# Three pad tiles between SBUF pools, and a state space recursion by pairs and fours, in a two-block network kernel

## The chip, the cores and the metric

The kernel runs on one core of a Trainium2 chip. One launch computes everything. The metric is the device time of one execution in microseconds (us); 1,995.99 us is the median of three runs before the change (1,995.98 to 1,996.63).

## The reference

The input is a sequence of 256 tokens with 1,024 features, in float32. A first block has a state space mixer with a gated projection, a squared-ReLU MLP and a gated additive projection. A second block of two layers has four mixers side by side (Fourier, convolution, grouped attention, differential attention) over the sequence and a context of 256 tokens, each followed by a SwiGLU MLP. Cut to what the change touches:

```python
def s5_mixer(u, ...):                      # u: (1, 256, 1024), 64 groups of 16 features, 64 complex states each
    ab = exp(lam * dt)                     # complex, per group and state
    bu = einsum('blgh,gph->blgp', ug, bb)  # input to each state
    xs = scan over l:  xs[l] = ab * xs[l-1] + bu[l]
    y  = real(einsum('blgp,ghp->blgh', xs, c)) + d_skip * u
    a, g = split(gelu(y) @ w_glu)
    return a * sigmoid(g)

def sqrelu_mlp(h, w1, w2):  a = relu(h @ w1); return (a * a) @ w2
def swiglu(h, w1, w3, w2):  return (silu(h @ w1) * (h @ w3)) @ w2
```

## The kernel before

**The projections.** Activations are kept with the features on the 128 partitions and the tokens along the row. Each float32 operand is split into a high part (rounded to the type that TensorE multiplies in one pass, `fp32r`) and a low part. A product takes three matmuls for each 128 features: high weights by high activations (L363), high by low (L364), low by high (L365), all in `mm3`; `mm3x` (L372 to L374) does the same for two units in turn. The weights come by DMA into `ws` tiles, are split by ScalarE (L331) and VectorE (L332) into `wh` and `wl` of pool `wr`, and are the stationary operand; 256 or 512 tokens move. In the token projections (`tok_wide`, L1029 to L1031) it is the other way round: activations are stationary and 512 weight columns move.

**Where tiles lie.** `run` opens the pools one after another, and each lies behind the one before in every partition: `c`, `sm`, `p1` (tiles `k1`, 1,024 bytes), `p2` (`k2`, 2,048 bytes), `p4` (`k4`, 4,096 bytes). Then the pools of the state space stage are opened and closed, and in their place come `ws` (3 tiles of 4,096 bytes), `wr` (4 each of `wh` and `wl`, 4,096 bytes), `up` (one tile of 4 x 286 floats), `ph` (`h4`, six of 4,096 bytes) and `late`. `Act` is the class of activations with a high and a low part; it takes its tiles from `k4` unless told otherwise. From `k4` come `y`, `h` and `g` of the first block, all `m`, and the mixers' results `zg`, `z`, `zd`, `zc`. From `ph` come `hc` of the first layer and `hx` of both; the `h` of the two SwiGLUs has its high parts in `ph` and its low parts in `k4`.

**The state space stage.** The 256 tokens are 32 chunks of 8. Within a chunk a Toeplitz matrix (`kt`, spread by 32 transfers into `mt`) gives the output (L739); across chunks the state at each chunk's start is needed. `s5_params` computes the powers of `ab`. `b_outer` builds the products that turn a chunk of inputs into its state contribution, PE applies them (L660) and ScalarE copies the contributions into `zb` (L670). A loop of 30 steps then runs the recursion across chunks on VectorE, four instructions a step on 2 x 32 columns (L677 to L680), with copies that swap the real and imaginary halves of `zb` after steps 23 and 30 (L686 to L688). `c_outer` builds the tap products `ca` on VectorE (L780, L782) and GpSimd (L781, L782); PE makes `kt` from them (L708, L714), ScalarE copies it (L716), SP and GpSimd issue the `mt` transfers (L720). Last, `zb` times `ca` is added to the output (L751).

**Order.** The program is written in the order of the functions; the framework's scheduler places each engine's instructions by program order and by when it takes their inputs to be ready, so `c_outer` and the recursion are interleaved on VectorE. L739 is held before L751 with `issue_after`, and the first loads behind the stage (`ple_proj`) are issued after the last `mt` transfer on SP.

Of the kernel before, what the change touches and what calls it, by code (L numbers as in the profile page):

```python
# [9 lines left out]
F32 = mybir.dt.float32  # L10
# [3 lines left out]
ALU = mybir.AluOpType  # L14
# [3 lines left out]
P = 128  # L18
# [260 lines left out]
class Net:  # L279
# [216 lines left out]
    def s5_params(self):  # L496
# [80 lines left out]
                f, g = slice(64 * half, 64 * half + 64), slice(32 * half, 32 * half + 32)  # L577
                self.S.copy(self.bb3[r, g, 0::2], bb[f, ri].unsqueeze(2).to_broadcast([64, 32, 2, 16]))

        arr, aii = (self.q6.tile([P, 2, 32], F32, name=s) for s in ("arr", "aii"))  # L580
        for r in range(2):
            V.tensor_copy(arr[:, r, :], pr[:, :, 0])
        V.tensor_scalar(aii[:, 0, :], pi[:, :, 0], -1.0, None, op0=ALU.mult)
        V.tensor_copy(aii[:, 1, :], pi[:, :, 0])
        self.arr, self.aii = arr, aii

    def b_outer(self, dst, g0, xr, xi):

# [15 lines left out]
    def s5(self):  # L604
# [13 lines left out]
        sh = [P, 32, 32]  # L618
# [20 lines left out]
        for h in range(2):  # L639
            G.memset(mt[h], 0.0)  # L640
        zb = self.q6.tile([P, 2, 32, 32], F32, name="zb")
        V.memset(zb[:, :, :, 0:1], 0.0)
        bre, bim = self.bb[:, 0], self.bb[:, 1]
        for jp in range(4):
            ss_sb = self.k4([P, 2, 2, 2, 64], F32, "ss")
            for jj in range(2):
                pt = self.q4.tile([P, 4, 2, 8, 16], F32, tag="pt", name=self.nm("pt"))
                self.b_outer(pt, (jp * 2 + jj) * 4, bre, bim)
                self.ada_next(2)
                pmt = self.k4([P, 4, 2, P], F32, "pmt")  # L650
                for g2 in range(2):
                    ps = self.pm([P, 4, P])
                    for i in range(4):
                        g4, ri = g2 * 2 + i // 2, i % 2
                        T.transpose(ps[:, i, :], pt[:, g4, ri].rearrange("p s h -> p (s h)"), self.ident)
                    S.copy(pmt[:, g2 * 2 : g2 * 2 + 2].rearrange("p a b c -> p (a b) c"), ps)
                ps = self.px([P, 2, 2, 64])
                for half in range(2):
                    for g4 in range(4):
                        T.matmul(ps[32 * g4 : 32 * g4 + 32, half], u2[half][:, g4 * 8 + jp * 2 + jj, :],  # L660
                                 pmt[:, g4, :, half * 64 : half * 64 + 64], start=True, stop=True)
                S.copy(ss_sb[:, jj], ps.rearrange("p a b c -> p b a c"))
            ps = self.px([P, 2, 2, 4, 32])
            for jj in range(2):
                for ri in range(2):
                    T.transpose(ps[:, jj, ri].rearrange("p a b -> p (a b)"),
                                ss_sb[:, jj, ri].rearrange("p a b -> p (a b)"), self.ident)
            for jj in range(2):
                g0 = (jp * 2 + jj) * 4
                S.copy(zb[:, :, g0 : g0 + 4, 1:32], ps[:, jj, :, :, 0:31])  # L670


        for s in range(1, 31):
            prev, nxt = zb[:, :, :, s], zb[:, :, :, s + 1]
            t1 = self.sm([P, 2, 32])
            t2 = self.sm([P, 2, 32])
            V.tensor_tensor(t1, prev, self.arr, op=ALU.mult)  # L677
            V.tensor_tensor(t2, zb[:, ::-1, :, s], self.aii, op=ALU.mult)
            V.tensor_tensor(t1, t1, nxt, op=ALU.add)
            V.tensor_tensor(nxt, t1, t2, op=ALU.add)  # L680
            if s in (23, 30):

                c = slice(0, 24) if s == 23 else slice(24, 32)
                t = self.bb.rearrange("p a (b e) c -> p (a b) (e c)", e=2)
                cp = V.tensor_copy if s == 23 else S.copy
                cp(t[64:128, :, c], zb[0:64, 1, :, c])  # L686
                V.tensor_copy(zb[0:64, 1, :, c], zb[64:128, 0, :, c])
                cp(zb[64:128, 0, :, c], t[64:128, :, c])  # L688


        ca = {}
# [1 line left out]
        for j in range(8):  # L693
            c = self.k4([P, 8, 8, 16], F32, "ca")
            for g0 in (0, 4):
                self.c_outer(c[:, g0 : g0 + 4], j * 8 + g0, c1, c2)
            self.ada_next()
            ca[j] = c


        for half in range(2):
# [40 lines left out]
        for half in range(2):  # L742
            y = ysb[half] = self.k4([P, 8, 8, 16], F32, "ysb")
            for jq in range(2):
                ps = pss[half, jq]
                with self.tc.issue_after(last.ins):
                    for j4 in range(4):
                        j = jq * 4 + j4
                        for g4 in range(4):
                            g = j * 4 + g4  # L750
                            T.matmul(ps[32 * g4 : 32 * g4 + 32, j4].rearrange("p s h -> p (s h)"), zb[:, half, g, :],  # L751
                                     ca[half * 4 + g // 8][:, g % 8].rearrange("p s h -> p (s h)"), start=False, stop=j4 == 3)
                (V.tensor_copy if jq else S.copy)(y[:, :, jq * 4 : jq * 4 + 4].rearrange("p s j h -> p j s h"), ps)
        S.copy(self.x[:, 0, 0:1], ysb[0][:, 0, 0, 0:1])
# [845 lines left out]
    def run(self):  # L1600
        tc, nc = self.tc, self.nc
        V, S, G = self.V, self.S, self.G
        with ExitStack() as st:
# [4 lines left out]
            self.ps_ = pool("sm")  # L1608
            self.p1 = pool("p1")
            self.p2 = pool("p2")  # L1610
            self.p4 = pool("p4")
            self.psm = pool("psm", 3, space=PSUM)
            self.psx = pool("psx", space=PSUM)
# [32 lines left out]
                nc.scalar.dma_start(self.rope.rearrange("p a b c -> p (a b c)"), self.a["rope"])  # L1646
            self.stage, self.ada_off = self.k4, 0
            self.ws = pool("ws", 3)
            self.wr = pool("wr", 4)
            self.up = pool("up", 1)  # L1650
            self.ph = pool("ph", NH)
            pl = pool("late")
            self.late = {"k4a": pl, "k1c": pl, "k1g": pl}
# [115 lines left out]
```

## Time and profile before

| | |
|---|---|
| median of three runs | 1,995.99 us |
| profiled execution | 1,997.63 us |
| its span, first to last instruction | 1,995.9 us |
| PE busy | 96% |
| DVE busy | 78% |
| ACT busy | 46% |
| POOL busy | 7% |
| mean granted TensorE clock | 0.985 of full speed |
| DMA | 162 GB/s on average |

PE is TensorE, DVE VectorE, ACT ScalarE, POOL GpSimd, SP the engine that issues most transfers. A matmul's duration runs from its issue to its modelled end, and the next one starts before it ends; so the distance between two starts is the time that one takes in the stream, and the duration is not. Where a line of the timeline ends in brackets, they hold the idle time ahead of it and what ended it.

### The profile page before, as it was taken

What the parts mean: (1) busy time and instruction counts of PE and PEld (TensorE: products, weight loads), DVE (VectorE), ACT (ScalarE), POOL (GpSimd) and SP (SyncE); (2) the same over time, 40 slices, a digit from 0 to 9 for tenths busy, and PEclk for the clock granted to TensorE, in tenths of its full rate; (3) what the DMA queues carried; (4) which work ended last, traced back from release to release, by engine and by line L of the source; (5) the groups of instructions that cost most, each with busy time, mean ns of one, the idle gap of its engine ahead of it and who ended that gap; (6) DMA issues with size and microseconds to landing.
All of it is one profiled execution on the core that took longest, in us unless ns stands there. A gap on an engine that the chain in (4) does not pass through costs nothing.

```text
span 1995.9 us, 35545 instructions
## 1 busy us (share of the span) xinstructions
PE 1906.2 (96%) x13842; PEld 1692.7 (85%) x13842; DVE 1548.6 (78%) x3133; ACT 927.4 (46%) x1583; POOL 130.9 (7%) x138
## 2 busy tenths in 40 slices
PE   3869999999999999999999999999999999999998
PEld 1457899998789998789998777787998789999997
DVE  9974577699987789998778576675689997776665
ACT  2443445455654555664553212212555664544443
POOL 6720000000000011000000000000100000010000
PEclk8989999999999999999999999999999999999998
DMA  5657665554345564236555455454455235555663
GB/s 176 187 187 244 224 199 183 180 183 156 106 125 169 182 191 156 88 106 189 181 187 157 126 163 164 152 165 124 141 178 157 74 108 170 180 180 169 183 187 107
DMA packets 103192, 323.45 MB, mean 162 GB/s; under 512 B 16416, under 2 KB 18608, under 8 KB 102640
## 3 DMA queue, kind: packets, MB, share of 16 engines
q1 hardware_dynamic: 102256, 319.53, 51.3%
q8 instruction: 109, 1.79, 0.4%
q0 software_dynamic: 336, 1.44, 0.2%
q14 instruction: 59, 0.48, 0.1%
q10 hardware_dynamic: 432, 0.21, 0.0%
HBM read 317.47 MB, written 1.05 MB: 160 GB/s over the span
## 4 chain that ended last, share of the span: by engine, by line
PE 84%; DVE 11%; issue 2%; DMA 2%; ACT 1%; SPq 0%; DVEq 0%; ACTq 0%
PE pm L363 21%; PE pm L364 21%; PE pm L365 21%; PE pm L1029 2%; PE pm L1031 2%; PE pm L1030 2%; DVE wl L332 2%; PE px L1351 1%; DVE cy L1060 1%; PE px L1300 1%; PE pm L372 1%; PE pm L373 1%; PE px L918 1%; PE pm L374 1%; PE px L1333 1%
## 5 line engine op out<-in xcount | busy, mean ns | idle before, releaser
L331 ACT CAST wh<-ws 128x1024 fp32r<-128x1024 f32 (+3 forms) x556 | 533.1, 961 | 723.7 <-PE pm L364 410.2
L332 DVE TENSOR_TENSOR wl<-ws,wh 128x1024 fp32r<-128x1024 f32 (+3 forms) x556 | 616.5, 1116 | 267.0 <-ACT wh L331 264.5
L363 PE MATMUL pm<-h,wh 128*128 128x256 f32 (+1 forms) x928 | 301.1, 324 | 0.0
L365 PE MATMUL pm<-h,wl 128*128 128x256 f32 (+1 forms) x928 | 299.5, 323 | 0.0
L364 PE MATMUL pm<-h,wh 128*128 128x256 f32 (+1 forms) x928 | 298.9, 322 | 0.0
L363 PE MATMUL pm<-m,wh 128*128 128x256 f32 (+1 forms) x704 | 213.7, 304 | 0.0
L364 PE MATMUL pm<-m,wh 128*128 128x256 f32 (+1 forms) x704 | 213.2, 303 | 0.0
L365 PE MATMUL pm<-m,wl 128*128 128x256 f32 (+1 forms) x704 | 212.6, 302 | 0.0
L363 PEld LDWEIGHTS pm<-h,wh 128*128 128x128 f32 x928 | 176.1, 190 | 20.7 <-ACT wh L331 4.6
L364 PEld LDWEIGHTS pm<-h,wh 128*128 128x128 f32 x928 | 176.2, 190 | 15.9 <-issue 0.8
L365 PEld LDWEIGHTS pm<-h,wl 128*128 128x128 f32 x928 | 175.7, 189 | 14.9
L363 PE MATMUL pm<-hx,wh 128*128 128x256 f32 x640 | 184.0, 288 | 0.0
L364 PE MATMUL pm<-hx,wh 128*128 128x256 f32 x640 | 180.6, 282 | 0.0
L365 PE MATMUL pm<-hx,wl 128*128 128x256 f32 x640 | 180.2, 281 | 0.0
L1060 DVE SCALAR_TENSOR_TENSOR cy<-up,vecs,cy 128x256 f32<-128x256 f32 x360 | 162.6, 485 | 1.4
L363 PEld LDWEIGHTS pm<-m,wh 128*128 128x128 f32 x704 | 134.1, 191 | 8.5 <-ACT wh L331 1.7
L364 PEld LDWEIGHTS pm<-m,wh 128*128 128x128 f32 x704 | 134.2, 191 | 6.6 <-issue 1.7
L952 DVE SCALAR_TENSOR_TENSOR ac<-wa,sc,ac 128x512 f32<-128x512 f32 x168 | 116.9, 747 | 27.6 <-DMA wa<-w_ada 27.6
L365 PEld LDWEIGHTS pm<-m,wl 128*128 128x128 f32 x704 | 134.2, 191 | 4.9
L429 POOL TENSOR_TENSOR ssq<-ssq,sq 128x256 f32<-128x256 f32 x45 | 43.2, 960 | 1429.2 <-ACT sq L423 1427.8
L363 PEld LDWEIGHTS pm<-hx,wh 128*128 128x128 f32 x640 | 121.1, 189 | 2.2 <-issue 2.0
L364 PEld LDWEIGHTS pm<-hx,wh 128*128 128x128 f32 x640 | 121.4, 190 | 0.3
(439 smaller groups left out, 4278.0 us busy)
## 6 DMA issues: line engine op xcount, KB each, us to landing
wa<-w_ada SPq DMA_DIRECT2D x96, 512.0 KB, 4.0
ws<-w_gp SPq DMA_DIRECT2D x96, 512.0 KB, 3.7
ws<-w_f SPq DMA_DIRECT2D x88, 512.0 KB, 4.4
ws<-w_tok SPq DMA_DIRECT2D x76, 512.0 KB, 4.0
ws<-mlp_w SPq DMA_DIRECT2D x64, 512.0 KB, 4.1
ws<-w_gp SPq DMA_DIRECT2D x96, 256.0 KB, 2.7
ws<-w_f2a SPq DMA_DIRECT2D x32, 512.0 KB, 4.4
ws<-w_cin SPq DMA_DIRECT2D x24, 512.0 KB, 4.5
```

Source lines behind the costliest of these rows:

```text
L331: self.S.copy(hi, src)
L332: self.V.tensor_tensor(lo, src, hi.bitcast(F32), op=ALU.subtract)
L363: self.T.matmul(out, h, ah, start=start and i == 0, stop=False)
L364: self.T.matmul(out, h, al, start=False, stop=False)
L365: self.pe_last = self.T.matmul(out, l, ah, start=False, stop=stop and i == n - 1)
L372: self.T.matmul(out, wh, act.hi(k), start=k == 0, stop=False)
L429: (eng or self.G).tensor_tensor(acc, acc, sq, op=ALU.add)
L952: V.scalar_tensor_tensor(acc[:, v], st[:, i], c, acc[:, v], op0=ALU.mult, op1=ALU.add)
L1029: self.T.matmul(ps, hi, a, start=k == 0, stop=False)
L1030: self.T.matmul(ps, lo, a, start=False, stop=False)
L1031: self.pe_last = self.T.matmul(ps, hi, b, start=False, stop=k == KC - 1)
L1060: V.scalar_tensor_tensor(y[:, k], up[:, k, i : i + L], w[:, i : i + 1], y[:, k], op0=ALU.mult, op1=ALU.add)
```

## The change

Three tiles that nothing reads are allocated: 24 floats (96 bytes) at the head of `p2`, 16 floats (64 bytes) at the head of `ws` and 24 floats (96 bytes) at the head of `up`. They shift the pools behind them.

The recursion is computed in another order. With the factor's first, second and fourth powers (made in `s5_params`), all odd chunks are first updated from their even neighbours, then every fourth from two back, then seven steps of four along every fourth chunk, then the rest of the odd ones from two back, and last the even ones from the odd ones. `zb` has chunk ahead of group now. The swap copies are gone: the odd chunks are copied by ScalarE, and the last additions write straight, into two new tiles `zf`, one for each half of the features, which L751 reads. The loop over `c_outer` now stands ahead of the recursion in the program.

```diff
--- before.py
+++ after.py
@@ -577,12 +577,62 @@
                 f, g = slice(64 * half, 64 * half + 64), slice(32 * half, 32 * half + 32)
                 self.S.copy(self.bb3[r, g, 0::2], bb[f, ri].unsqueeze(2).to_broadcast([64, 32, 2, 16]))
 
-        arr, aii = (self.q6.tile([P, 2, 32], F32, name=s) for s in ("arr", "aii"))
-        for r in range(2):
-            V.tensor_copy(arr[:, r, :], pr[:, :, 0])
-        V.tensor_scalar(aii[:, 0, :], pi[:, :, 0], -1.0, None, op0=ALU.mult)
-        V.tensor_copy(aii[:, 1, :], pi[:, :, 0])
-        self.arr, self.aii = arr, aii
+        self.am = []
+        wr, wi = pr[:, :, 0], pi[:, :, 0]
+        for j in range(3):
+            arr, aii = (self.q6.tile([P, 2, 32], F32, name=f"{s}{j}") for s in ("arr", "aii"))
+            if j:
+                t, u = q32(), q32()
+                V.tensor_tensor(t, wi, wi, op=ALU.mult)
+                V.tensor_tensor(u, wr, wr, op=ALU.mult)
+                V.scalar_tensor_tensor(aii[:, 1, :], wr, 2.0, wi, op0=ALU.mult, op1=ALU.mult)
+                V.tensor_tensor(arr[:, 0, :], u, t, op=ALU.subtract)
+            else:
+                V.tensor_copy(arr[:, 0, :], wr)
+                V.tensor_copy(aii[:, 1, :], wi)
+            wr, wi = arr[:, 0, :], aii[:, 1, :]
+            V.tensor_copy(arr[:, 1, :], wr)
+            V.tensor_scalar(aii[:, 0, :], wi, -1.0, None, op0=ALU.mult)
+            self.am.append((arr, aii))
+
+    def s5_step(self, zb, dst, src, level):
+
+        V = self.V
+        arr, aii = self.am[level]
+        n = len(range(32)[dst])
+        sh = [P, 2, n, 32]
+        arr, aii = (v.unsqueeze(2).to_broadcast(sh) for v in (arr, aii))
+        new = self.k4 if n > 8 else self.k2 if n > 1 else self.sm
+        t1, t2 = new(sh, F32, "t1"), new(sh, F32, "t2")
+        V.tensor_tensor(t1, zb[:, :, src], arr, op=ALU.mult)
+        V.tensor_tensor(t2, zb[:, ::-1, src], aii, op=ALU.mult)
+        V.tensor_tensor(t1, t1, zb[:, :, dst], op=ALU.add)
+        return t1, t2
+
+    def s5_scan(self, zb):
+
+
+        V, S = self.V, self.S
+
+        def add(dst, src, level):
+            t1, t2 = self.s5_step(zb, dst, src, level)
+            V.tensor_tensor(zb[:, :, dst], t1, t2, op=ALU.add)
+
+        zf = [self.k4([P, 32, 32], F32, "zf") for _ in range(2)]
+        add(slice(1, 32, 2), slice(0, 32, 2), 0)
+        add(slice(3, 32, 4), slice(1, 32, 4), 1)
+        for c in range(7, 32, 4):
+            add(slice(c, c + 1), slice(c - 4, c - 3), 2)
+        add(slice(5, 32, 4), slice(3, 29, 4), 1)
+        t1, t2 = self.s5_step(zb, slice(2, 32, 2), slice(1, 31, 2), 0)
+        for half in range(2):
+            f = slice(64 * half, 64 * half + 64)
+            for ri in range(2):
+                r = slice(64 * ri, 64 * ri + 64)
+                S.copy(zf[half][r, :, 1::2], zb[f, ri, 1::2].rearrange("p c g -> p g c"))
+                V.tensor_tensor(zf[half][r, :, 2::2].rearrange("p g c -> p c g"), t1[f, ri], t2[f, ri], op=ALU.add)
+            V.memset(zf[half][:, :, 0:1], 0.0)
+        return zf
 
     def b_outer(self, dst, g0, xr, xi):
 
@@ -639,7 +689,7 @@
         for h in range(2):
             G.memset(mt[h], 0.0)
         zb = self.q6.tile([P, 2, 32, 32], F32, name="zb")
-        V.memset(zb[:, :, :, 0:1], 0.0)
+        V.memset(zb[:, :, 0:1, :], 0.0)
         bre, bim = self.bb[:, 0], self.bb[:, 1]
         for jp in range(4):
             ss_sb = self.k4([P, 2, 2, 2, 64], F32, "ss")
@@ -667,25 +717,7 @@
                                 ss_sb[:, jj, ri].rearrange("p a b -> p (a b)"), self.ident)
             for jj in range(2):
                 g0 = (jp * 2 + jj) * 4
-                S.copy(zb[:, :, g0 : g0 + 4, 1:32], ps[:, jj, :, :, 0:31])
-
-
-        for s in range(1, 31):
-            prev, nxt = zb[:, :, :, s], zb[:, :, :, s + 1]
-            t1 = self.sm([P, 2, 32])
-            t2 = self.sm([P, 2, 32])
-            V.tensor_tensor(t1, prev, self.arr, op=ALU.mult)
-            V.tensor_tensor(t2, zb[:, ::-1, :, s], self.aii, op=ALU.mult)
-            V.tensor_tensor(t1, t1, nxt, op=ALU.add)
-            V.tensor_tensor(nxt, t1, t2, op=ALU.add)
-            if s in (23, 30):
-
-                c = slice(0, 24) if s == 23 else slice(24, 32)
-                t = self.bb.rearrange("p a (b e) c -> p (a b) (e c)", e=2)
-                cp = V.tensor_copy if s == 23 else S.copy
-                cp(t[64:128, :, c], zb[0:64, 1, :, c])
-                V.tensor_copy(zb[0:64, 1, :, c], zb[64:128, 0, :, c])
-                cp(zb[64:128, 0, :, c], t[64:128, :, c])
+                S.copy(zb[:, :, 1:32, g0 : g0 + 4].rearrange("p r c g -> p r g c"), ps[:, jj, :, :, 0:31])
 
 
         ca = {}
@@ -696,6 +728,8 @@
                 self.c_outer(c[:, g0 : g0 + 4], j * 8 + g0, c1, c2)
             self.ada_next()
             ca[j] = c
+
+        zf = self.s5_scan(zb)
 
 
         for half in range(2):
@@ -748,7 +782,7 @@
                         j = jq * 4 + j4
                         for g4 in range(4):
                             g = j * 4 + g4
-                            T.matmul(ps[32 * g4 : 32 * g4 + 32, j4].rearrange("p s h -> p (s h)"), zb[:, half, g, :],
+                            T.matmul(ps[32 * g4 : 32 * g4 + 32, j4].rearrange("p s h -> p (s h)"), zf[half][:, g, :],
                                      ca[half * 4 + g // 8][:, g % 8].rearrange("p s h -> p (s h)"), start=False, stop=j4 == 3)
                 (V.tensor_copy if jq else S.copy)(y[:, :, jq * 4 : jq * 4 + 4].rearrange("p s j h -> p j s h"), ps)
         S.copy(self.x[:, 0, 0:1], ysb[0][:, 0, 0, 0:1])
@@ -1608,6 +1642,8 @@
             self.ps_ = pool("sm")
             self.p1 = pool("p1")
             self.p2 = pool("p2")
+
+            self.p2.tile([P, 24], F32, tag="pad", bufs=1, name="pad2")
             self.p4 = pool("p4")
             self.psm = pool("psm", 3, space=PSUM)
             self.psx = pool("psx", space=PSUM)
@@ -1646,8 +1682,10 @@
                 nc.scalar.dma_start(self.rope.rearrange("p a b c -> p (a b c)"), self.a["rope"])
             self.stage, self.ada_off = self.k4, 0
             self.ws = pool("ws", 3)
+            self.ws.tile([P, 16], F32, tag="pad", bufs=1, name="pads")
             self.wr = pool("wr", 4)
             self.up = pool("up", 1)
+            self.up.tile([P, 24], F32, tag="pad", bufs=1, name="padu")
             self.ph = pool("ph", NH)
             pl = pool("late")
             self.late = {"k4a": pl, "k1c": pl, "k1g": pl}
```

## Rows read from the trace of the kernel before

**Rows 1.** The page: busy engines, and the chain that ended last, by line.

```profile
PE 1906.2 (96%) x13842; PEld 1692.7 (85%) x13842; DVE 1548.6 (78%) x3133; ACT 927.4 (46%) x1583; POOL 130.9 (7%) x138
...
PE pm L363 21%; PE pm L364 21%; PE pm L365 21%; PE pm L1029 2%; PE pm L1031 2%; PE pm L1030 2%; DVE wl L332 2%; PE px L1351 1%; DVE cy L1060 1%; PE px L1300 1%; PE pm L372 1%; PE pm L373 1%; PE px L918 1%; PE pm L374 1%; PE px L1333 1%
```

**Rows 2.** Counts: L363 and L1029 over the span, then L363 by operand and shape.

```profile
0.00:1996.00 1996.00, 958.84 (x3184) 0.99 0.52 162
...
0.00:1996.00 1996.00, 109.86 (x272) 0.99 0.52 162
...
L363 PE MATMUL pm<-hx,wh 128*128 128x256 f32 x640 | 184.0, 288 | 0.0
L363 PE MATMUL pm<-h,wh 128*128 128x512 f32 x336 | 133.3, 397 | 0.0
L363 PE MATMUL pm<-hc,wh 128*128 128x256 f32 x320 | 91.8, 287 | 0.0
L363 PE MATMUL pm<-m,wh 128*128 128x512 f32 x128 | 50.3, 393 | 0.0
```

**Rows 3.** Timeline of PE in four stages: start, duration (us), first and last shown.

```profile
260.12 0.28 PE L363 MATMUL pm<-m,wh 128*128 128x256 f32 x1
...
260.84 0.28 PE L363 MATMUL pm<-m,wh 128*128 128x256 f32 x1
...
1479.82 0.28 PE L363 MATMUL pm<-hx,wh 128*128 128x256 f32 x1
...
1480.88 0.28 PE L363 MATMUL pm<-hx,wh 128*128 128x256 f32 x1
...
1175.76 0.39 PE L365 MATMUL pm<-m,wl 128*128 128x512 f32 x1
...
1176.67 0.39 PE L363 MATMUL pm<-m,wh 128*128 128x512 f32 x1
...
1199.98 0.39 PE L364 MATMUL pm<-h,wh 128*128 128x512 f32 x1
...
1201.38 0.39 PE L364 MATMUL pm<-h,wh 128*128 128x512 f32 x1
```

**Rows 4.** Timeline of PE: eight transposes in a row.

```profile
501.57 1.04 PE L1252 MATMUL px<-ident,zq 128*128 128x128 f32 x8
```

**Rows 5.** Groups of instructions up to 135 us: busy us, mean ns, idle before.

```profile
L677 DVE TENSOR_TENSOR sm<-zb,arr 128x64 f32<-128x64 f32 x30 | 11.5, 384 | 0.7
L678 DVE TENSOR_TENSOR sm<-zb,aii 128x64 f32<-128x64 f32 x30 | 11.2, 373 | 0.0
L679 DVE TENSOR_TENSOR sm<-sm,zb 128x64 f32<-128x64 f32 x30 | 10.1, 336 | 0.0
...
L456 DVE SCALAR_TENSOR_TENSOR e<-e,e 128x32 f32<-128x32 f32 x12 | 2.3, 188 | 0.1
```

**Rows 6.** Timeline of DVE: instructions of known size, two starts of one step.

```profile
55.77 0.69 DVE L599 TENSOR_TENSOR pt<-pt,ta 128x512 f32<-128x512 f32 x1
...
106.99 0.27 DVE L677 TENSOR_TENSOR sm<-zb,arr 128x64 f32<-128x64 f32 x1
...
107.96 0.27 DVE L677 TENSOR_TENSOR sm<-zb,arr 128x64 f32<-128x64 f32 x1
...
133.07 2.35 DVE L332 TENSOR_TENSOR wl<-ws,wh 128x1024 fp32r<-128x1024 f32 x2
```

**Rows 7.** Timeline of all engines: the end of the state space stage.

```profile
91.42 24.19 SPq L720 DMA_DIRECT2D mt<-kt  x27
...
106.49 0.58 ACT L716 COPY kt<-px 128x512 f32<-128x512 f32 x1 [4.49 <-PE px L714]
...
118.49 1.13 PE L739 MATMUL px<-mt,u 128*32 128x128 f32 x24
...
127.34 0.27 DVE L680 TENSOR_TENSOR zb<-sm,sm 128x64 f32<-128x64 f32 x1
...
128.91 4.35 PE L751 MATMUL pm<-ca,zb 128*32 128x128 f32 x96 [9.29 <-ACT zb L688]
```

## The prediction

> **What bounds the kernel now.** I read the page first: TensorE is busy for 96% of the span, VectorE for 78%, and of the chain of waits that ended last three lines, L363 to L365, hold 63%; with the token projections L1029 to L1031 (2% each) it is 69% [rows 1], or 1,377 us of 1,995.9. These are the three passes (high by high, high by low, low by high) of every projection. So two things set the time: the rate at which these matmuls follow each other, and a front part in which DVE prepares the state space mixer while PE waits.
>
> A busy share cannot tell the rate, since a matmul of 0.28 us overlaps the next. The distance of their starts in the timeline can. With 256 columns and activations from the `k4` pool the starts go from 260.12 to 260.84 in six steps: 0.120 us each [rows 3]. With the activations `hx`, which lie in the pool `ph`, 1479.82 to 1480.88 in nine steps: 0.118 us (0.1178) [rows 3]. With 512 columns, `m` from `k4`: 1175.76 to 1176.67 in four, 0.2275 us; `h`, whose high half is in `ph`: 1199.98 to 1201.38 in six, 0.2333 us [rows 3]. No row in these runs shows a wait, so something per matmul differs by stage. What the stages differ in, beside the tile names, is the place of the activations. The pools are stacked in the order in which they are opened, and all tiles from `p4` to `wr` are multiples of 128 bytes, so `k4` activations and the weights in `wr` have the same remainder mod 128. The one `up` tile of 4 x 286 floats is 4,576 bytes, 35 x 128 + 96, so `ph` begins 96 bytes on: 32 bytes from the weights mod 128, in the other direction. That the remainder is the cause is an inference; two stages at different places can differ by something else.
>
> **The pads.** The three tiles are 96, 64 and 96 bytes. The first moves `k2`, `k4` and all behind them; the second moves `wr` 64 further than `k4`; the third moves `ph` and `late` by 96 more, so `ph` stands 96 + 96 = 192, or 64 mod 128, from the weights. Every operand pair of L363 to L365 and L1029 to L1031 is then 64 apart. No row of before shows that distance. How many matmuls it touches: L363 has 3,184, of which 336 + 128 have 512 columns [rows 2], which leaves 2,720, and 8,160 for three lines. Of these `hx` and `hc` are 960 x 3 = 2,880 from `ph` [rows 2], and the second layer's feed-forward `h` (22 x 2 x 8 less the 16 of its first unit, 336) has its high half there, which two of the three passes read: 672. So 3,552 run 32 apart and 4,608 at equal remainders. With 512 columns: 384 of `m` at equal remainders, and 1,008 of `h` (mixed) and 272 x 3 = 816 of L1029 to L1031 [rows 2], 1,824 for which I use 0.2333.
>
> Bounds. Below: eight 128-column transposes take 1.04 us, one alone about 0.27, so 0.110 us each [rows 4]; there the weight load of 128 columns sets the pace, and each of our matmuls has one too. 0.110 for 256 columns and, at the same rate, 0.220 for 512 would save 4,608 x 10 ns + 3,552 x 7.8 + 384 x 7.5 + 1,824 x 13.3 = 101 us. Above: from 0 to 32 bytes the 512-column matmul lost 5.8 ns; another such step for 64 costs 384 x 11.6 + 1,824 x 5.8 = 15 us, and for 256 columns I go as far over 0.120 as 32 lies under it, 0.122: 9 + 15 = 24 us; together 39 us worse. Since the chain holds 1,377 us of the 1,484 that these matmuls take (553 + 418 + 87 + 426), I count 93%: from -94 to +36 us. I take 0.116 for 256 columns, another step like that from 0 to 32, and 0.230 for the 1,824, half way from 0.2333 to the better row, with `m` unchanged: 18.4 + 6.4 + 6.0 = 30.8, on the chain 29 us.
>
> The row that bears on this is the pair 0.120 and 0.118 of [rows 3], both at full clock by the page's slices. The Trainium skill (SBUF — State Buffer, "Who interferes with whom") says that TensorE reads moving operand and weights through two independent ports and never waits on anyone; by that the pads are worth nothing. The trace does not settle it: it shows two rates, but not that the remainder makes them.
>
> What hides nothing here: DVE and ACT must split the weights faster too, but DVE is busy 78% [rows 1], so a stream 2% shorter leaves it slack over most stages; in the attention stages, where DVE is fuller, part of the gain is lost, which is the 7% not counted.
>
> **The recursion.** Now: 30 steps of four DVE instructions on 64 elements. Undisturbed, a step is 107.96 - 106.99 = 0.97 us [rows 6], 29.1 us for 30; then three copies midway that swap halves, at most 0.69 each as 512 elements take [rows 6], and a tail from the last update (127.34 + 0.27) to 128.91 [rows 7]: 3 us, in all 32. Beside POOL's work the instructions stretch: mean 384, 373 and 336 ns [rows 5] against 260 undisturbed, (124 + 113 + 76) x 30 = 9.4 us. After: a level-0 pair update on 1,024 elements, 4 x 1.17 (two such take 2.35) [rows 6] = 4.7 us; level 1 on 512, 4 x 0.69 [rows 6] = 2.8; seven serial steps by fours, 7 x 0.97 = 6.8; the 448 element update, 2.8 at most; three instructions on 960, 3.5; four merging adds of 480 elements, 2.8, and two memsets, 0.4. Sum 23.8, so 8 us less. Twelve small instructions are added for the squared and fourth powers: 12 x 0.19 [rows 5] = 2.3 us, early, where DVE also leads. The taps' products now come before the scan in program order. Of the new scan only some eight long instructions can fall beside POOL's products, each stretched by about the 0.7 us that the small ones show, 5 to 6 us against 9.4: 4 us gained. 8 - 2.3 + 4 = 10 us.
>
> What is late next: the second half's `mt` transfers. The last `kt` copy is at 106.49 on ACT, SP's 27 issues end at 115.6, and the matmuls L739 that wait for them end at 119.6 (118.49 + 1.13); the recursion lets PE go on at 128.91 [rows 7]. With `kt` unmoved L751 could start near 119.6, 9 us earlier; `kt` should come earlier since the products that feed it are no longer interleaved with 30 steps. Behind these transfers on SP stand the loads of `pt`, `ple_w` and `w_glu`, which move with them. The four copies to `zf` on ACT wait for DVE's updates; behind them are the first weight casts, which stood behind the swap copies too, so no new queue. The copy into `zb` now writes 128 bytes apart; the recursion read at that step without loss (64 elements in 0.26 us), so nothing is charged. The tiles fit: two `u`, eight `ca`, two `zf` and two products are the 14 buffers. Bounds: 0 if the scan runs wholly behind the products, which end near 105.6, just ahead of the last `kt` copy (105.6 + 23.8 = 129.4), 15 if `kt` comes 7 us earlier and DVE is never stretched.
>
> **The sum.** The profiled execution took 1,997.63 us, 1.7 over its span; the median of the runs is 1,995.99, so I take differences from that: 1,996 - 29 - 10 = 1,957 us.
>
> **Rivals.** (1) The pads do nothing: the rate belongs to the stage and not to the remainder, or 64 apart is like 0. For: equal remainders are the better case at 512 columns and the worse at 256, so there is no single trend. Against: each rate is steady within its stage. At no change 1,986 us; if all go to the rates of equal remainders, 3,552 x 2.2 - 1,824 x 5.8 = -3 us, 1,983. (2) Slower: 64 apart is worse than 32, the upper bound above: the loss falls on each of the 10,368 matmuls, +36 - 10 = 2,022 us. For: 512 columns lose 5.8 ns from 0 to 32. Against: 256 columns gain 2.2. It decides the sign from 14 us of loss on the chain, some 1.5 ns per matmul. (3) The scan does not shorten, since the products keep DVE until 105.6 and its levels follow each other; with the pads idle too: 1,996, with them 1,967.
>
> **How the numbers follow.** Forecast (the pads gain something, the scan gains): 0.58, itself 1,895 to 1,980. Rival 1: 0.22. Rival 2: 0.11. Rival 3: 0.06 with idle pads, 0.03 with working ones. A measurement of this kernel tells about 0.2%, 4 us, from no change. Faster: 0.58 + 0.22 + 0.03 = 0.83; within 0.2%: 0.06; slower: 0.11. The range is 1,905 to 2,000: it leaves out rival 2 and the last of the forecast's lower end, towards 1,996 - 94 - 15 = 1,887.
>
> **What would show it.** The starts of L363 to L365 in `m` stages: 0.116 us right, 0.120 rival 1, over 0.121 rival 2. For 512 columns 0.230 or less. In the front part L751 should start near 119 instead of 128.91, with the `kt` copies before 106.49; if it starts at 128 or later the scan's step failed. The forecast is wrong if the 256-column distance is unchanged or if L751 has not moved.

## The result: half of the forecast gain

| | before | after |
|---|---|---|
| median of the runs | 1,996.31 us (1,995.98 to 1,999.2) | 1,977.14 us (1,973.71 to 1,981.05) |
| profiled execution, its span | 1,997.63, 1,995.9 us | 1,976.91, 1,975.1 us |
| ratio | | 0.9898, interval 0.9885 to 0.991 |

By the ratio the change takes 20.4 us off (1.02% of 1,996.31); the medians differ by 19.2. The forecast was 1,957 us, 39 us less; the measured time lies within the range of 1,905 to 2,000. Two later runs (below), one with the pads alone and one with the recursion alone, give 0.9% and 0.2%; their sum, 1.1%, is the whole within the intervals.

The page after, busy engines and the chain by line, to compare with [rows 1]. Line numbers behind the recursion have moved by 34: L1063 to L1065 were L1029 to L1031.

```profile
PE 1890.5 (96%) x13842; PEld 1674.2 (85%) x13842; DVE 1547.0 (78%) x3070; ACT 931.8 (47%) x1585; POOL 135.5 (7%) x138
...
PE pm L363 20%; PE pm L364 19%; PE pm L365 19%; DVE wl L332 4%; PE pm L1063 2%; PE pm L1065 2%; PE pm L1064 2%; DVE cy L1094 2%; PE px L1385 2%; PE px L1334 1%; PE px L952 1%; PE pm L372 1%; PE pm L373 1%; PE px L1367 1%; PE pm L374 1%
```

PE still is the bound. Its three passes hold 58% of the chain where they held 63%: DVE's weight split L332 went from 2% to 4%, so it ends last in more places.

**The stream.** Timeline of PE after in four stages, first and last start of a stretch without a pause, to compare with [rows 3].

```profile
343.73 0.28 PE L363 MATMUL pm<-m,wh 128*128 128x256 f32 x1
...
346.11 0.28 PE L363 MATMUL pm<-m,wh 128*128 128x256 f32 x1
...
1158.76 0.39 PE L364 MATMUL pm<-m,wh 128*128 128x512 f32 x1
...
1161.80 0.39 PE L365 MATMUL pm<-m,wl 128*128 128x512 f32 x1
...
1183.02 0.39 PE L364 MATMUL pm<-h,wh 128*128 128x512 f32 x1
...
1186.93 0.39 PE L363 MATMUL pm<-h,wh 128*128 128x512 f32 x1
...
1464.84 0.28 PE L365 MATMUL pm<-hx,wl 128*128 128x256 f32 x1
...
1467.32 0.28 PE L365 MATMUL pm<-hx,wl 128*128 128x256 f32 x1
```

`m` with 256 columns: 21 steps in 2.38 us, 0.1133 us each where it was 0.120. `hx`: 21 steps in 2.48, 0.1181, as before. `m` with 512 columns: 13 steps in 3.04, 0.2338, worse than the 0.2275 of before. `h` with 512: 17 steps in 3.91, 0.2300, better than 0.2333. It is not the clock; the windows of after around two of these stages have it granted in full (1.00, ahead of the DMA share):

```profile
340.00:357.00 17.00, 17.00 (x151) 16.84 (x150) 12.13 (x15) 7.28 (x7) 0.00 (x0) 1.00 0.57 188
1462.00:1480.00 18.00, 18.00 (x155) 18.00 (x154) 14.53 (x23) 8.62 (x11) 0.00 (x0) 1.00 0.68 214
```

**The front part.** Timeline of after where the state space stage ends, to compare with [rows 7]: SP's transfers, ACT's last `kt` copy, the matmuls that wait for the transfers (L773, was L739), the merging adds, and the matmuls that wait for the recursion (L785, was L751).

```profile
93.31 21.80 SPq L754 DMA_DIRECT2D mt<-kt  x27
...
105.16 0.59 ACT L750 COPY kt<-px 128x512 f32<-128x512 f32 x1 [4.58 <-PE px L748]
...
118.12 1.47 PE L773 MATMUL px<-mt,u 128*32 128x128 f32 x24
...
121.96 4.18 DVE L633 TENSOR_TENSOR zf<-t,t 64x480 f32<-64x480 f32 x4
...
124.08 5.23 PE L785 MATMUL pm<-ca,zf 128*32 128x128 f32 x96 [4.49 <-DVE zf L633]
```

L785 starts at 124.08 instead of 128.91, 4.8 us earlier, not 10; the recursion still ends last (the wait is on `zf` L633). The `kt` copy is 1.3 us earlier, and PE's L773 still ends at 119.6.

What DVE does ahead of it in after: the taps' products by turns with POOL, then the scan, of which some starts are shown.

```profile
72.42 2.65 DVE L814 TENSOR_TENSOR ca<-s5v,pr 128x448 f32<-128x448 f32 x2
...
79.59 2.85 DVE L814 TENSOR_TENSOR ca<-s5v,pr 128x448 f32<-128x448 f32 x2
80.75 2.50 POOL L815 TENSOR_TENSOR ta<-s5v,pi 128x448 f32<-128x448 f32 x2
82.36 1.36 DVE L816 TENSOR_TENSOR ca<-ca,ta 128x448 f32<-128x448 f32 x1
83.20 1.52 POOL L816 TENSOR_TENSOR ca<-ca,ta 128x448 f32<-128x448 f32 x1
83.65 2.85 DVE L814 TENSOR_TENSOR ca<-s5v,pr 128x448 f32<-128x448 f32 x2
...
102.45 2.16 DVE L607 TENSOR_TENSOR t<-zb,arr 128x1024 f32<-128x1024 f32 x1
...
110.89 0.22 DVE L607 TENSOR_TENSOR t<-zb,arr 128x64 f32<-128x64 f32 x1
...
111.68 0.23 DVE L607 TENSOR_TENSOR t<-zb,arr 128x64 f32<-128x64 f32 x1
```

A loop over two groups of taps takes 83.65 - 79.59 = 4.06 us, and while a product of POOL runs, one of DVE takes 1.36 to 1.43 us. The scan starts only at 102.45, wholly behind the products, and ends with the merges at 121.96 + 4.18 = 126.14: 23.7 us.

### The profile page after: what moved, and what is told of

Same layout as the page of the kernel before. It is cut to its first block, busy times and chain, and to the rows that moved or that the text cites. A ratio compares the mean times of both kernels' runs of the same rounds, so it can differ in the third digit from the quotient of the medians.

```text
span 1975.1 us, 35492 instructions
## 1 busy us (share of the span) xinstructions
PE 1890.5 (96%) x13842; PEld 1674.2 (85%) x13842; DVE 1547.0 (78%) x3070; ACT 931.8 (47%) x1585; POOL 135.5 (7%) x138
## 4 chain that ended last, share of the span: by engine, by line
PE 80%; DVE 14%; issue 2%; DMA 2%; ACT 2%; DVEq 0%; ACTq 0%; SPq 0%
PE pm L363 20%; PE pm L364 19%; PE pm L365 19%; DVE wl L332 4%; PE pm L1063 2%; PE pm L1065 2%; PE pm L1064 2%; DVE cy L1094 2%; PE px L1385 2%; PE px L1334 1%; PE px L952 1%; PE pm L372 1%; PE pm L373 1%; PE px L1367 1%; PE pm L374 1%
## 5 line engine op out<-in xcount | busy, mean ns | idle before, releaser
L332 DVE TENSOR_TENSOR wl<-ws,wh 128x1024 fp32r<-128x1024 f32 (+3 forms) x556 | 615.7, 1115 | 253.4 <-ACT wh L331 250.8
L363 PE MATMUL pm<-h,wh 128*128 128x256 f32 (+1 forms) x928 | 298.9, 322 | 0.0
L363 PE MATMUL pm<-m,wh 128*128 128x256 f32 (+1 forms) x704 | 211.2, 300 | 0.0
L364 PE MATMUL pm<-m,wh 128*128 128x256 f32 (+1 forms) x704 | 210.7, 300 | 0.0
L363 PEld LDWEIGHTS pm<-h,wh 128*128 128x128 f32 x928 | 175.0, 189 | 20.8 <-ACT wh L331 4.6
L363 PE MATMUL pm<-hx,wh 128*128 128x256 f32 x640 | 182.5, 285 | 0.0
L363 PEld LDWEIGHTS pm<-m,wh 128*128 128x128 f32 x704 | 132.1, 188 | 9.3 <-ACT wh L331 1.7
L364 PEld LDWEIGHTS pm<-m,wh 128*128 128x128 f32 x704 | 132.4, 188 | 7.6 <-issue 1.7
L363 PEld LDWEIGHTS pm<-hx,wh 128*128 128x128 f32 x640 | 120.2, 188 | 2.2 <-issue 2.0
L365 PEld LDWEIGHTS pm<-hx,wl 128*128 128x128 f32 x640 | 120.3, 188 | 0.0
```

What stands on the lines that cost most here:

```text
L332: self.V.tensor_tensor(lo, src, hi.bitcast(F32), op=ALU.subtract)
L363: self.T.matmul(out, h, ah, start=start and i == 0, stop=False)
L364: self.T.matmul(out, h, al, start=False, stop=False)
L365: self.pe_last = self.T.matmul(out, l, ah, start=False, stop=stop and i == n - 1)
```

## The experiments

Theory: the distance between the start addresses of activations and weights, modulo 128 bytes, sets the rate of the stream, and DVE's line of work sets the front part. (That the distance does it came out; that 128 is the period did not, as the run with 80 bytes shows.) The rivals: the rate belongs to the stage or to the absolute place; the recursion's order, and not its length, is what counts. Mean distances below are worked out from all starts of PE in a trace together with the addresses of the program, pauses (over 150 ns with 256 columns, over 260 with 512) left out. "`k4`" and "`ph`" are the pools of the moving activations; weights are in `wr`. Where a distance is given modulo 256, it is the start of the moving operand less the start of the stationary one.

**Pads alone.** The kernel before with the three pads of the change.

```diff
+            self.p2.tile([P, 24], F32, tag="pad", bufs=1, name="pad2")
+            self.ws.tile([P, 16], F32, tag="pad", bufs=1, name="pads")
+            self.up.tile([P, 24], F32, tag="pad", bufs=1, name="padu")
```

> The kernel before with the three pads alone. Theory (the remainder of the addresses mod 128 sets the pace of the matmuls): 256-column matmuls of the stages with k4 activations go from 0.120 us to a mixture of 0.113 and 0.118 (mean near 0.1157), those with ph activations from 0.118 to near 0.1175; L751 still starts near 128.9 us; time 1977 to 1982, some 15 to 18 us under before. Rival (the pace comes from when the stages are entered, which the new recursion shifted, and not from addresses): 0.120 as before and a time within 4 us of 1996.

Measured: 1,981.28 us, ratio 0.9909 (0.9894 to 0.9925), 18.2 us of 1,998.65. The means fell to 115.9 ns (`k4`) and 117.5 (`ph`) from 119.5 and 118.2; with 512 columns `k4` rose from 229.0 to 231.8 and `ph` fell from 233.3 to 230.6. The pads carry nearly all of the gain.

**Recursion alone.** The changed kernel with the three pad lines taken out.

> The changed kernel without its three pads. Theory: matmul starts at 0.120 us again in the k4 stages, the front part ends some 4 us earlier than before (the output matmuls of the recursion start near 124 instead of 128.9), time 1991 to 1993. Rival (the pace comes from the shifted timing): 0.113 to 0.118 remains and the time stays near 1977.

Measured: 1,995.84 us, ratio 0.9982 (0.9972 to 0.9993): 3.6 us. The time itself is above the expected 1,991 to 1,993, but the kernel before ran at 1,998.65 beside it, and the expected gain of some 4 us came. The rates are those of before to 0.1 ns with 256 columns. Timelines, first of the run with the pads alone (the old recursion: first product, last `zb` copy, L751), then of this one:

```profile
68.79 2.65 DVE L780 TENSOR_TENSOR ca<-s5v,pr 128x448 f32<-128x448 f32 x2
...
127.63 0.29 DVE L687 COPY zb<-zb 64x256 f32<-64x256 f32 x1 [0.52 <-ACT bb L686]
...
128.41 0.87 PE L751 MATMUL pm<-ca,zb 128*32 128x128 f32 x12 [7.30 <-ACT zb L688]
```

```profile
123.13 4.58 PE L785 MATMUL pm<-ca,zf 128*32 128x128 f32 x96 [5.52 <-DVE zf L633]
```

With the old recursion DVE needs 127.92 - 68.79 = 59.1 us for products and recursion together, in after 126.14 - 72.42 = 53.7: 5.4 less. The products start 3.6 us later there, behind the squared and fourth powers, so DVE ends 1.8 us earlier. And PE begins once the merges of the first half are done, 2.1 us ahead of DVE's end, where L751 began 0.5 behind it: 1.8 + 2.1 + 0.5 is the 4.3 us between 128.41 and 124.08.

**Scan ahead of the products.** The changed kernel with one line moved.

```diff
+        zf = self.s5_scan(zb)
         ca = {}
...
-        zf = self.s5_scan(zb)
```

> The changed kernel with the new recursion written ahead of the loop over the tap products, as the old one stood. Theory (the gain of the recursion was cut to 4 us because it runs wholly behind the tap products, 102.5 to 126 us on VectorE): the scan is interleaved with the products, VectorE's total is the same but the long instructions cover GpSimd's idle waits; the output matmuls start between 118 and 124 and the time is 2 to 6 us under the changed kernel. Rival (VectorE is busy throughout either way, and GpSimd's products and the scan only exchange places; the last transfers into mt come later instead): no change, or some us slower, 1977 to 1985.

Measured: 2,005.07 us, ratio 1.0029 (1.0018 to 1.0041), 26 us slower than the changed kernel by the two ratios. My theory expected a gain and was wrong; the rival named what happens, but its 1,977 to 1,985 was too small as well. The timeline of this run:

```profile
80.77 1.23 DVE L607 TENSOR_TENSOR t<-zb,arr 128x1024 f32<-128x1024 f32 x1 [10.61 <-ACT zb L720]
...
106.04 1.16 DVE L814 TENSOR_TENSOR ca<-s5v,pr 128x448 f32<-128x448 f32 x2
...
123.27 22.92 SPq L754 DMA_DIRECT2D mt<-kt  x27
...
149.19 1.48 PE L773 MATMUL px<-mt,u 128*32 128x128 f32 x20
150.26 0.42 PE L785 MATMUL pm<-ca,zf 128*32 128x128 f32 x1
```

DVE idles 10.61 us for ACT's `zb`, and the products wait until 106.04. Behind the products comes a long tail (matmuls, `kt` copies, 27 transfers, L773), behind the scan only L785; so L773 ends 31 us later than in after (150.67 against 119.59). Products first is right.

**All pairs 32 bytes apart.** One 32-byte tile ahead of the weights: `k4` stays where it was and the weights move, so the stages of `m` come to the distance that `hx` had (224 modulo 256).

```diff
+            self.ws.tile([P, 8], F32, tag="pad", bufs=1, name="pads")
```

> The kernel before with one pad of 32 bytes ahead of the weights, which puts all activations of both pools 32 bytes from the weights mod 128. Theory (the difference decides): k4 stages take the pace that the ph stages had before, starts 0.116 to 0.122 apart, mean near 0.118, the 512-column matmuls of m go from 0.2275 to 0.233; time about 1988 to 1992. Rival (the pool or the absolute start decides): k4 stages stay at 0.120 (k4 has not moved) and the time stays at 1996.

Measured: 1,998.51 us, ratio 0.9995 (0.9984 to 1.0006). `m` with 256 columns fell to 118.3, with 512 it rose to 233.3, the values of `ph` before. So the rates came as the theory said; the time missed its 1,988 to 1,992 and is that of the kernel before. From the means and counts some 5.9 us were gained in the `k4` stages with 256 columns and 3.0 lost in those with 512; what is left, about 3 us, is at the edge of the interval. Timeline of PE, the stage of [rows 3] at 260 us, 20 steps of 0.118:

```profile
259.94 0.28 PE L363 MATMUL pm<-m,wh 128*128 128x256 f32 x1
...
262.30 0.28 PE L365 MATMUL pm<-m,wl 128*128 128x256 f32 x1
```

**All pairs at equal remainders.** One 32-byte tile behind `up`, which moves `ph` alone.

```diff
+            self.up.tile([P, 8], F32, tag="pad", bufs=1, name="padu")
```

> The kernel before with one pad of 32 bytes in the pool up alone: all activations and the weights at the same remainder mod 128. Theory (the difference decides): ph stages go from a mixture of 0.116 to 0.122 to 0.120, the 512-column matmuls with ph operands from 0.2333 to 0.2275 to 0.229; 3,520 x 1.6 ns lost, about 1,180 x 5 ns gained, time within 3 us of 1996. Rival (the pool or its absolute start decides): the 512-column matmuls of ph stay near 0.233.

Measured: 2,004.06 us in one run, the kernel before at 1,998.24 beside it. `hx` rose to 119.9 and `h` with 512 columns fell from 233.3 to 227.1. Timeline of PE in the stages of `m` and `hx`, 20 steps of 0.120 in both:

```profile
259.93 0.28 PE L364 MATMUL pm<-m,wh 128*128 128x256 f32 x1
...
262.33 0.28 PE L363 MATMUL pm<-m,wh 128*128 128x256 f32 x1
...
1478.90 0.28 PE L363 MATMUL pm<-hx,wh 128*128 128x256 f32 x1
...
1481.30 0.28 PE L365 MATMUL pm<-hx,wl 128*128 128x256 f32 x1
```

With the last run this shows the cause: a stage takes the rate of its distance, whichever operand is moved, and the 256- and the 512-column matmuls want opposite things. Two things do not fit so neatly. The time missed "within 3 us of 1,996": the rates make up about 1 us of the 5.8 lost, and where the rest went is open. And the stages of `zg`, `zd` and `zc`, which lie in `k4` at 0 bytes and run between groups on `hc` and `hx` from `ph`, went from 118.8 to 120.0 ns though only `ph` was moved. So a stage does not have its rate from its own distance alone; that it keeps something of the group ahead of it would fit, and was not tested.

**64 apart at other places.** Pads of 64, 64 and 96 bytes, so that the pairs start at 0 and 64 mod 128 instead of 32 and 96.

```diff
+            self.p2.tile([P, 16], F32, tag="pad", bufs=1, name="pad2")
+            self.ws.tile([P, 16], F32, tag="pad", bufs=1, name="pads")
+            self.up.tile([P, 24], F32, tag="pad", bufs=1, name="padu")
```

> The kernel before with pads of 64, 64 and 96 bytes: all pairs 64 apart as in the changed kernel, but activations start at 0 and weights at 64 mod 128 instead of 32 and 96. Theory (only the difference counts): the same as with the three pads alone, starts of 256 columns in two rhythms, 0.113 and 0.118, time 1977 to 1983. Rival (starts at 32 mod 64 matter): another mean than 0.1157 in the k4 stages, by over 1 ns, and a time off by 5 us or more.

The rates came as the theory said (115.7 and 117.4; 231.8 and 230.5): both operands 32 bytes away from their places in the changed kernel change nothing, so the distance counts, not the place. The time, 1,988.31 in one run, missed the expected 1,977 to 1,983. The starts of L363 show that the gain stood at 8.7 us at the 2,201st (1,432 us) and at 2.3 at the 2,301st (1,622 us). In that stretch the granted clock fell: PE was busy for 10.07 of 12 us, then ran for 10 us near half clock, 1.2 GHz (windows of this run: PE busy comes first, the clock ahead of the DMA share).

```profile
1425.00:1437.00 12.00, 10.07 (x89) 9.88 (x88) 10.89 (x19) 7.55 (x14) 4.13 (x4) 1.00 0.60 181
1437.00:1447.40 10.40, 10.23 (x40) 9.47 (x41) 6.27 (x21) 2.42 (x5) 0.11 (x1) 0.51 0.36 111
```

In the traces of before and after the clock is granted in full from 1,000 to 1,700 us. Ten us at half clock are worth about 5 us (an estimate from the row), most of the 6.4 lost. ACT's longest wait for a weights buffer that PE had not freed lies in the same stretch (timeline of ACT), at least in part behind the slower PE:

```profile
1449.91 1.05 ACT L331 CAST wh<-ws 128x1024 fp32r<-128x1024 f32 x1 [9.26 <-PE pm L1009]
```

**The `ws` pad alone.** 64 bytes between `k4` and the weights, which leaves `ph` 32 apart (192 and 224 modulo 256).

```diff
+            self.ws.tile([P, 16], F32, tag="pad", bufs=1, name="pads")
```

> The kernel before with the 64-byte pad ahead of the weights alone: k4 activations 64 from the weights, ph activations 32 as before. Theory: k4 stages as in the changed kernel, mean near 0.1157; ph stages as before, mean 0.118, 512 columns of ph at 0.233; time 1979 to 1984, most of the pads' gain, since the third pad is worth about 3,520 x 0.75 ns and some 2 us at 512 columns. Rival (the gain needs all three pads, since the operands of one stage interact): k4 stages near 0.118, time over 1988.

Measured: 1,987.92 us in one run, some 10 us gained, above the expected 1,979 to 1,984. `k4` went to 115.4, `ph` stayed at 118.5, as the theory says; `h` with 512 columns kept its slow rate (234.1). So one pad has more than half of the gain of the three, as far as one run tells. Of the other two, the pad in `up` moves `ph`; the one in `p2` moves `k4`, the weights and `ph` alike, so it changes no distance between them.

**80 bytes apart.** The changed kernel with the weights 16 bytes further, 48 from the activations the other way. The edit does more than that: each weights tile grows by 128 bytes, so the four buffers, which were a multiple of 256 bytes apart, now are 4,224 apart, and units in turn stand at 48 and at 176 bytes modulo 256. Modulo 128 the two are the same.

```diff
-            hi = self.wr.tile([P, m], F32R, tag="wh", name=self.nm("wh"))
-            lo = self.wr.tile([P, m], F32R, tag="wl", name=self.nm("wl"))
+            hi = self.wr.tile([P, m + 32], F32R, tag="wh", name=self.nm("wh"))[:, 4 : m + 4]
+            lo = self.wr.tile([P, m + 32], F32R, tag="wl", name=self.nm("wl"))[:, 4 : m + 4]
```

> The changed kernel with the weights tiles moved by 16 bytes more: both halves of every weights unit start 112 mod 128, all activations 32, so all pairs lie 80 bytes apart (48 the other way) instead of 64. Theory that exactly half of 128 is the best place and neighbours lie on a slope from 0 (120) over 32 (118.3) to 64 (113.3 or 117.7): starts of 256 columns between 115.7 and 118.3 ns, near 117, time 1980 to 1988 us. Rival that the two locked rhythms belong to exactly 64 and a place beside it always finds the better one: 113.3 ns alone, some 8,600 x 3 ns = 20 to 25 us off the changed kernel, 1952 to 1957 us. Rival that 16 bytes change nothing: 1974 to 1981.

Measured: 1,989.4 us, ratio 0.9956 (0.994 to 0.9973); the time is a little above the expected range, the rate in it. `k4` 117.8, `ph` 118.0, with 512 columns 232.8 and 232.1. These are means of two rates. The stage of `m`, three first matmuls of a unit, 24 steps from one to the next: 0.1188 us at 176 bytes, then 0.1167 at 48.

```profile
346.22 0.28 PE L363 MATMUL pm<-m,wh 128*128 128x256 f32 x1
...
349.07 0.28 PE L363 MATMUL pm<-m,wh 128*128 128x256 f32 x1
...
351.87 0.28 PE L363 MATMUL pm<-m,wh 128*128 128x256 f32 x1
```

All the stretches of 20 or more matmuls on one unit in this trace divide so, in `k4` and `ph` alike: over a hundred at 48 bytes have means of 116.5 to 117.2 ns, over a hundred at 176 have 118.2 to 119.5. Units 256 bytes apart (48 and 304, 176 and 432) go alike, units 128 apart do not. So the period is not 128 bytes; 256 fits all runs. Then 64 bytes to one side and to the other are two places: in the change `k4` stands at 192 modulo 256 and `ph` at 64. With 256 columns the means are 119.9 (0 bytes, the run at equal remainders), 117.0 (48), 117.5 (64), 118.8 (176), 115.7 (192) and 118.3 (224): no slope towards half of 128, and 192 is the best place tried. No run has 128, or moving activations from `ph` at 192.

**Taps' products on VectorE alone.** The changed kernel, GpSimd out of `c_outer`.

```diff
-        G.tensor_tensor(ta, c2[:, g, :].unsqueeze(2).to_broadcast(sh), pi, op=ALU.mult)
-        (G if g0 % 8 else V).tensor_tensor(c[:, :, 0:7], c[:, :, 0:7], ta, op=ALU.add)
+        V.tensor_tensor(ta, c2[:, g, :].unsqueeze(2).to_broadcast(sh), pi, op=ALU.mult)
+        V.tensor_tensor(c[:, :, 0:7], c[:, :, 0:7], ta, op=ALU.add)
```

> The changed kernel with the tap products wholly on VectorE instead of shared with GpSimd. Theory (the two engines take turns on the products: a pair on VectorE takes 2.85 us beside GpSimd and 1.16 alone, so eight loops of 4.06 us are the sum of both engines' work): six products of 0.53 us are 3.2 us a loop, the loop over taps shrinks from 30 to 26 us or less, the recursion starts and ends 4 us earlier, time 3 to 5 us under the changed kernel. Rival (the sharing gains what it should and VectorE becomes the longer one): 48 products on VectorE alone end no earlier, time unchanged or longer.

Measured: 1,972.42 us, ratio 0.987 (0.9853 to 0.9886). Timeline of this run: SP's transfers, one group's products, the last `kt` copy, the matmuls that wait for the transfers, and L785.

```profile
93.28 20.74 SPq L754 DMA_DIRECT2D mt<-kt  x27
...
93.33 0.62 DVE L815 TENSOR_TENSOR ta<-s5v,pi 128x448 f32<-128x448 f32 x1
93.87 0.62 DVE L814 TENSOR_TENSOR ca<-s5v,pr 128x448 f32<-128x448 f32 x1
94.41 0.62 DVE L816 TENSOR_TENSOR ca<-ca,ta 128x448 f32<-128x448 f32 x1
94.94 0.62 DVE L815 TENSOR_TENSOR ta<-s5v,pi 128x448 f32<-128x448 f32 x1
...
100.48 0.58 ACT L750 COPY kt<-px 128x512 f32<-128x512 f32 x1 [0.86 <-PE px L748]
...
114.22 0.61 PE L773 MATMUL pm<-mt,u 128*32 128x128 f32 x2 [3.24 <-DMA mt<-kt]
...
117.80 0.35 PE L785 MATMUL pm<-ca,zf 128*32 128x128 f32 x2
```

A group takes 94.94 - 93.33 = 1.61 us on VectorE alone, two take 3.2 where the shared loop took 4.06: VectorE now issues six instructions per loop instead of three, and is done sooner. L785 starts at 117.80, 11.1 us earlier than before, and the wait ahead of it is now that of L773 for the transfers. This is the 10 us that the forecast had promised for the front part; they came by another step than it named. In time the run is 4.7 us under the changed kernel, as expected; the two ratios' intervals just touch (0.9853 to 0.9886 and 0.9885 to 0.991). The Trainium skill (SBUF — State Buffer, "Who interferes with whom") says that a VectorE instruction with two inputs in SBUF contends with a GpSimd instruction that reads SBUF; the trace agrees: one such instruction is 1.36 us long beside POOL and 0.62 alone.

**The outer products `b_outer` too.** On top of it, the two products of `b_outer` moved to VectorE.

```diff
-        G.tensor_tensor(ta, xi, pi, op=ALU.mult)
+        V.tensor_tensor(ta, xi, pi, op=ALU.mult)
...
-        G.tensor_tensor(tb, xr, pi, op=ALU.mult)
+        V.tensor_tensor(tb, xr, pi, op=ALU.mult)
```

> The changed kernel with the taps' products (c_outer) and the outer products of b_outer wholly on VectorE, GpSimd none of them. If two-input instructions of the two engines delay each other, as the taps' loops showed (25.7 us on VectorE alone for the sixteen against 32.5 shared), the eight b_outer calls gain too: 6 x 0.60 us on VectorE against loops of about 4.1 us now, at most 8 x 0.5 = 4 us, less where PE's transposes and not VectorE set the pace there. Theory: 1968 to 1972 us, first y matmul at 129 to 132 us (132.4 with only the taps moved). Rival: GpSimd's half is real help in b_outer, since there VectorE has other work too (the normalisation): 1972 to 1977, first y after 132.4.

Measured: 1,970.36 us, ratio 0.9862 (0.9843 to 0.988). That interval lies below that of the change; against the run with the taps alone the two overlap and nothing is told. The first matmul on `y` starts at 133.3, no earlier than with the taps alone (132.4), which speaks for the rival, though the time lies in the range of the theory. Timeline of this run, one `b_outer` and L785:

```profile
55.21 0.69 DVE L647 TENSOR_TENSOR pt<-bb,pr 128x512 f32<-128x512 f32 x1 [3.10 <-PE pm L705]
...
118.53 4.96 PE L785 MATMUL pm<-ca,zf 128*32 128x128 f32 x96 [4.57 <-DVE zf L633]
```

DVE now is ahead and waits for buffers that PE's transposes L705 hold. It has the lowest median of all versions.

## Why the prediction was half right

**The cause of the rate: right in the distance, wrong in the period.** The distance between the two operands' starts sets the rate: moving only the weights or only `ph` moved the rates of the stages concerned, and another absolute place changed nothing. Rival 1 (the pads do nothing) and rival 2 (64 is worse) fell. But the prediction counted distances modulo 128, by which every pair would be "64 apart"; by the run with 80 bytes 128 is not the period, and `k4` (192 modulo 256) and `ph` (64) came to different places. By what the Trainium skill says (SBUF — State Buffer, "Who interferes with whom"), that TensorE reads through two independent ports and never waits on anyone, the pads would be worth nothing. They were worth 18.2 us, and the measurement decides: the same instructions at the same clock run at 0.120 or at 0.1133 by the placing of tiles alone. Whether the two reads meet or something else inside the chip does this, no run shows.

**The size, term by term.** The forecast held 18.4 + 6.4 + 6.0 = 30.8 us of stream. Measured, mean distance by count:

| term | forecast | measured |
|---|---|---|
| 256 columns from `k4` | 4 ns, 18.4 us | 119.5 to 115.7, x 4,880 = 18.7 us |
| 256 columns from `ph` | 1.8 ns, 6.4 us | 118.2 to 117.5, x 3,531 = 2.7 us |
| 512 columns, moving operand in `ph` | 3.3 ns, 3.3 us | 233.3 to 230.6, x 660 = 1.8 us |
| 512 columns of L1063 to L1065 | 3.3 ns, 2.7 us | 233.0 to 233.3, x 519 = -0.2 us |
| 512 columns from `k4` | 0 | 229.0 to 231.8, x 703 = -2.0 us |

That is 21.0 us, of which the run with the pads alone gave 18.2, 87% instead of the 93% counted. The failing terms are `ph` and the 512 columns. I took one value, 0.116, for all 256-column pairs, since I took all to be at one distance. They are at two: at 192 modulo 256 the mean is 115.7, at 64 it is 117.5, so `ph` gained 0.7 ns and not 1.8. It is not the pool: where the weights move (L1042 to L1044 of after) pairs with `ph` stand at 192 and have 113.9, those with `k4` stand at 64 and have 117.9. That 115.7 met the 0.116 was luck: it is a mixture of stages at 0.1133 and at 0.118, and no row of before showed the first. And the row that should have warned me stood in [rows 3]: 512 columns did better at equal remainders (0.2275) than at 32 (0.2333), so leaving `m` unchanged was a free choice on the wrong side.

**The recursion: the step on the order failed.** The scan's length was forecast at 23.8 us and took 23.7, with errors that cancel: the level on 1,024 elements took 5.8 us instead of 4.7, four merges 4.18 instead of 2.8, the seven serial steps 0.79 each instead of 0.97. But L785 came at 124.08, not near 119. The term "less stretching beside POOL, 4 us" is what failed: the products and POOL's share of them kept DVE until 102.45, so the scan ran wholly behind them, as the bound of 0 and rival 3 had it, and the long instructions of the products are stretched as the small steps were. The products started 3.3 to 3.6 us later, where 2.3 were counted for the new parameters: four of the twelve instructions (L588, L589) took 1.06 us on the mean, not 0.19. Rival 3 was not right either, as it had the recursion gain nothing: the scan as a whole is shorter than 30 steps, and PE starts on the first half early. With the recursion alone 3.6 us were measured, where 10 were forecast.

**What was late next** was named rightly but did not decide until GpSimd was taken out: then the `mt` transfers end last, and L785 starts at 117.80.

The sum: 18.2 (pads, 29 forecast) + 3.6 (recursion, 10 forecast) = 21.8, against 20.4 measured for both.

## What to carry to other kernels

Where a stream of matmuls bounds a kernel, read the distance of starts stage by stage and hold it against the addresses of both operands (modulo 256 bytes, as far as these runs tell): an unused tile can be worth 1%, but each shape must be measured, since what helps 256 columns can cost 512. Before splitting two-input products between VectorE and GpSimd, compare a loop beside the other engine with the sum of its instructions alone; here the split was a loss. And of two jobs on one engine, the one with the longer tail of other engines behind it goes first.

## What the hardware showed that was not expected

- At 192 bytes modulo 256 a stage without pauses keeps one of two rhythms, 0.1133 us or 0.1178; after a pause it may be in the other. Which one it takes is not in the addresses: the 21 steps of `m` from 343.73 that took 2.38 us in after took 2.47 with the taps on VectorE, the same matmuls at the same addresses (first and last, that run):

```profile
334.85 0.28 PE L363 MATMUL pm<-m,wh 128*128 128x256 f32 x1
...
337.32 0.28 PE L363 MATMUL pm<-m,wh 128*128 128x256 f32 x1
```

  Over all `k4` stages that run has a mean of 116.3 ns where after has 115.7, 3 us of time. What chooses the rhythm, and whether it differs between executions of one kernel, stayed open. At 64 nine steps in ten are near 0.118 (`hx` from 1464.84); at equal remainders there is one rhythm, 0.120, in a stream that is at equal remainders throughout.
- The distance acts on 512 columns the other way: 0.227 at 0 bytes, about 0.233 at 32 to either side, 0.230 to 0.234 at 64 to either side.
- VectorE alone is faster at these two-input products (1.61 us a group) than VectorE and GpSimd together (2.03).
